# z, B, C, x and V of a hybrid layer by seven products, with their token sums held on chip

## The chip, the cores and the metric

The kernel runs on one core of a Trainium2 chip. The metric is the device time of one execution in microseconds (us), median of several runs. TensorE (PE) does matmuls and transposes; its weight loads (PEld) run beside them. VectorE (DVE), ScalarE (ACT) and GpSimd (POOL) do the elementwise work; SyncE (SP) and POOL issue the transfers between device memory (DRAM) and the on-chip memory SBUF. Matmul results land in PSUM.

## The reference

One decoder layer for 1024 tokens of 1024 features, in float32. The input is normed, projected once, and goes through two mixers side by side: a state-space scan (16 heads in 2 groups) and a differential attention (8 heads). Both outputs go through one output projection; a gated feed-forward network (FFN) and a norm follow.

```python
n   = RMSNorm(h)
p   = n @ W_in            # one combined projection, columns split into [SSD z | SSD xBC | SSD dt | DA q | DA k | DA v]
y_s = SSD(p_ssd)          # causal depthwise conv on x/B/C, chunked SSD scan, D skip, SiLU(z)-gated grouped RMSNorm
y_a = DiffAttn(p_da)      # (softmax(q1k1) - lambda softmax(q2k2)) v, causal, NoPE, per-head RMSNorm * (1 - lambda_init)
h   = h + concat(y_s, y_a) @ W_out
h   = h + SwiGLU(RMSNorm(h))
```

z and x have 1024 columns each (512 for each group), B and C 128 per group, dt 16, and q, k and v 1024 each.

## The kernel before, in words

**Exact matmuls in three.** A float32 operand is split into a high part (a copy to the PE's own float type, on ACT, L172) and a low part (the rest, a subtraction on DVE, L173). `mm3` (L126 to L129) multiplies high by high, high by low and low by high into one PSUM sum. In the trace one such product is three lines, L127, L128 and L129.

**The prologue.** Eight tiles of 128 tokens are loaded, normed (L111 on DVE; for every second tile a part of the work on POOL, L108, and ACT), transposed (16 turns of four 128x128 transposes, L120) and split (L123 on ACT, L124 on DVE) into `nhi` and `nlo`: four tiles that stay in SBUF until attention's last projection.

**Stages.** (1) z of group 0 together with dt, in units of 264 columns (`proj_z0`), then the decays. (2) For each group: B, C and four tiles of x (`conv_tiles`, by `proj_T`: 128 columns stationary, 512 tokens moving), a convolution over four tokens on DVE and a SiLU; the scan's inputs CT, Bn, CB and xn stay in SBUF. (3) The scan over eight chunks of 128 tokens (`ssd_scan`), which is mostly DVE and ACT work; on PE z of group 1 (`proj_nat`: 128 tokens stationary, 256 columns moving) runs beside scan 0, and the first V, K and Q beside scan 1. (4) Attention: for each head `qk` (K and Q by `proj_T`), for each pair of heads `v_pair` (V by `proj_nat`), and for each head eight steps, one per query block: `att_front` (scores, mask L587, maximum L588, exponential L590, reciprocal L593, the combination L596), and one step later `att_back` (transposes, the product with V at L611). A step's elementwise chain goes DVE, ACT, DVE; PE fills its wait with projections of later heads. (5) The output projection, in four groups of 512 rows; its operand is loaded from DRAM, scaled by a column of `pcol` and split by ACT and DVE (L175, L176). (6) The FFN, whose gate, up and down products already use Winograd's scheme of seven half-size products for eight.

**Order.** The program lists the work stage by stage, and the language's scheduler then orders each engine's instructions by its own timeline, once, when the kernel is built (L1077). Pools with a fixed number of buffers limit it: `B16` 4, `A4` 14, `P4` 6, `CV` 4, `raw` 2, `wh` 3, `wl` 3, and two PSUM tiles each for `MM`, `SC` and `MS`.

Of the kernel before, what the change touches and what calls it, by code (L numbers as in the profile page):

```python
# [9 lines left out]
F32 = mybir.dt.float32  # L10
# [14 lines left out]
def tile_hybrid_block(  # L25
# [51 lines left out]
    cs_d = dram.tile([P, P], F32, name="cs_d")  # L77

# [15 lines left out]
    def norm_rows(parts, wbc, outs, name, pool=(), junk=None):  # L94
        """outs = RMSNorm of the row whose column pieces are parts; pieces in pool are weighted on Pool and scaled on ACT"""
# [16 lines left out]

    def norm_transpose(parts, wbc, his, los, t, xn, pts, name, pool=()):
        norm_rows(parts, wbc, [xn], name, pool)
        tk = slice((t % 4) * P, (t % 4) * P + P)
        for q in range(2):
            pt = pts([P, 4, P], f"pt_{name}_{q}")
            for j in range(4):
                k = q * 4 + j
                nc.tensor.transpose(pt[:, j, :], xn[:, k * P:(k + 1) * P], ident)  # L120
            hi = his[t // 4][:, q * 4:q * 4 + 4, tk]
            lo = los[t // 4][:, q * 4:q * 4 + 4, tk]
            nc.scalar.copy(hi, pt)  # L123
            nc.vector.tensor_tensor(lo, pt, hi.bitcast(F32), op=ALU.subtract)  # L124
# [45 lines left out]
    def split(hi, lo, raw, scale=None):  # L170
        if scale is None:
            nc.scalar.copy(hi, raw)  # L172
            nc.vector.tensor_tensor(lo, raw, hi.bitcast(F32), op=ALU.subtract)  # L173
# [84 lines left out]
    def proj_z0(us, name, sink):
        """units of 264 columns; sink(t, psum [128 tokens, 264])"""
        for t in range(NT):  # L260
            ps = (MS if t % 4 > 1 else MM)([P, 264], f"mm_{name}_{t}")
            tk = slice((t % 4) * P, (t % 4) * P + P)
            for k in range(KD):
                hi, lo = us[k // 4]
                mm3(ps, nhi[t // 4][:, k, tk], nlo[t // 4][:, k, tk], hi[:, k % 4, :], lo[:, k % 4, :],
                    k == 0, k == KD - 1)
            sink(t, ps)

    def proj_nat(col, name, sink):
        """256 columns; sink(t, psum [128 tokens, 2 blocks from t, 256])"""  # L270
        us = [w_unit(w_in_k[:, 4 * u:4 * u + 4, col:col + 256], [P, 4, 256], f"{name}_{u}") for u in range(2)]
        for t in range(0, NT, 2):
            ps = MM([P, 2, 256], f"mm_{name}_{t}")
            for i in range(2):
                tk = slice(((t + i) % 4) * P, ((t + i) % 4) * P + P)
                for k in range(KD):
                    hi, lo = us[k // 4]
                    mm3(ps[:, i, :], nhi[t // 4][:, k, tk], nlo[t // 4][:, k, tk], hi[:, k % 4, :], lo[:, k % 4, :],
                        k == 0, k == KD - 1)
            sink(t, ps)  # L280

# [14 lines left out]
    def decays():  # L296
# [13 lines left out]
        for c in (15, 13, 11, 9, 7, 5, 3):  # L310
# [6 lines left out]
                                       op0=ALU.mult, op1=ALU.mult)  # L317
        cps = MS([P, P], "cps")
# [16 lines left out]
    def conv_tiles(*tiles):  # L335
        jobs = []
        for ct, name, acc in tiles:
            u_ = CV([P, T], F32, "u_" + name)
# [4 lines left out]

        def sink_of(ct, name, acc, u_):
            def sink(half, ps):
                sl = slice(half * 512, half * 512 + 512)
# [4 lines left out]
        for ct, name, acc, u_ in jobs:
            for sh in (1, 2, 3):
                nc.vector.scalar_tensor_tensor(acc[:, sh:], u_[:, :T - sh], wk(ct, 3 - sh), acc[:, sh:],
                                               op0=ALU.mult, op1=ALU.add)
            nc.scalar.activation(acc, acc, AF.Silu)

    def gate_dt():
        """the gate of group 0 and dt"""
        for a in range(2):
            zt = [None]  # L360
            w0, w = (0, 248) if a == 0 else (248, 264)

            def sink(t, ps):
                if t % 2 == 0:
                    zt[0] = CV([P, 2, w], F32, f"zt0_{a}_{t}")
                if a == 0:
                    nc.vector.tensor_tensor(adt[:, t, :], ps[:, 0:16], hv[:, 0, :], op=ALU.add)
                nc.scalar.activation(zt[0][:, t % 2, :], ps[:, 264 - w:], AF.Silu)
                if t % 2 == 1:
                    nc.gpsimd.dma_start(z_d[t - 1:t + 1, :, w0:w0 + w].rearrange("t p c -> p t c"), zt[0])  # L370
            proj_z0(zus if a == 0 else [z0_unit(z0_raw(1, u), 1, u) for u in range(2)], f"z0_{a}", sink)

    def gate(g):
        for hf in range(2):
            zt = [None]
            zc = g * 512 + hf * 256

            def sink(t, ps):
                if t % 4 == 0:
                    zt[0] = CV([P, 4, 256], F32, f"zt{g}_{hf}_{t}")  # L380
                nc.scalar.activation(zt[0][:, t % 4:t % 4 + 2, :], ps, AF.Silu)
                if t % 4 == 2:
                    nc.gpsimd.dma_start(z_d[t - 2:t + 2, :, zc:zc + 256].rearrange("t p c -> p t c"), zt[0])
# [698 lines left out]
```

## Time and profile before

| what | value |
|---|---|
| median of 3 runs | 1643.95 us (1643.94 to 1646.22) |
| span of the profiled execution | 1643.3 us |
| PE busy | 1597.2 us, 97% |
| DVE busy | 1071.6 us, 65% |
| ACT busy | 775.8 us, 47% |
| POOL busy | 429.2 us, 26% |
| moved by DMA | 172.78 MB, 105 GB/s |

The profile lists groups of instructions by line, engine and tile: `out<-in`, the form, `x` count, then busy time and mean ns of one, then the idle time of the engine ahead of them and what ended it. `L127 PE MATMUL mm_z<-wh_z,nhi` is the first third of z's product. A window row gives, for a stretch of the span, the busy time of each engine with its instructions, the clock that PE was granted (1.00 is full), and the DMA engines' share. In time order the stages lie at 0 to 75 us (norm, z0, dt), to 151 (B, C, x of group 0), to 228 (scan 0 with z1), to 302 (B, C, x of group 1), to 395 (scan 1 with the first V, K and Q), to 718 (attention with projections) and to 865 (attention without projections, and the output projection's start).

### The profile page before, as it was taken

The page shows a single profiled execution, that of the slowest core. Times are in us where ns is not written, and L with a number is a line of the kernel's source. Part 1 is how long each engine was busy: PE and PEld are TensorE (multiplying, and loading weights), DVE is VectorE, ACT ScalarE, POOL GpSimd, SP SyncE. Part 2 cuts the span into 40 slices and gives each one's busy share as a digit, 9 for nine tenths or more (in the row PEclk, how much of TensorE's full clock was granted, in tenths as well). Part 3 has the DMA queues.
Part 4 walks back from the last instruction along what each step waited for, and adds up shares of the span by engine and source line. Part 5 has one row for each costly group of instructions (what it writes and reads, how often), then busy time and mean ns, then how long its engine had stood idle before and what let it go on. Part 6 is the DMA issues. An engine that isn't in the chain of part 4 may idle for free. (4 is left out here: it accounts for less than half of the span.)

```text
span 1643.3 us, 23716 instructions
## 1 busy us (share of the span) xinstructions
PE 1597.2 (97%) x9170; PEld 1386.9 (84%) x9170; DVE 1071.6 (65%) x1682; ACT 775.8 (47%) x1608; POOL 429.2 (26%) x378
## 2 busy tenths in 40 slices
PE   6999999999999999999999998999999999999997
PEld 6988878887989989889999987888888888778885
DVE  5345745688776676677674477455555555898987
ACT  6444764456555565575552245333333333334445
POOL 4100330032000000013300034444444443542322
PEclk9999999999999999999999999999999999999999
DMA  5321451143011110147523221233333323944122
GB/s 195 110 79 52 129 163 56 36 142 92 24 46 39 46 33 27 45 130 229 162 77 116 84 99 56 96 102 104 111 116 118 98 96 134 365 166 186 39 103 103
DMA packets 105291, 172.78 MB, mean 105 GB/s; under 512 B 7813, under 2 KB 75530, under 8 KB 103770
## 3 DMA queue, kind: packets, MB, share of 16 engines
q1 hardware_dynamic: 95210, 137.11, 25.2%
q0 software_dynamic: 9968, 34.15, 6.3%
q8 instruction: 72, 1.18, 0.3%
q14 instruction: 41, 0.34, 0.1%
HBM read 125.82 MB, written 45.42 MB: 104 GB/s over the span
## 5 line engine op out<-in xcount | busy, mean ns | idle before, releaser
L127 PE MATMUL x<-n,wa 128*128 128x512 f32 x352 | 138.7, 396 | 0.0
L128 PE MATMUL x<-n,wa 128*128 128x512 f32 x352 | 138.7, 394 | 0.0
L129 PE MATMUL x<-n,wa 128*128 128x512 f32 x352 | 137.8, 394 | 0.0
L590 ACT ACTIVATE p<-s,nmx 128x256 f32<-128x256 f32 (+7 forms) x128 | 94.4, 740 | 53.2 <-DVE nmx L588 49.9
L172 ACT CAST wa<-s 128x512 fp32r<-128x512 f32 x88 | 54.7, 622 | 132.3 <-PE x L129 59.4
L173 DVE TENSOR_TENSOR wa<-s,wa 128x512 fp32r<-128x512 f32 x88 | 76.8, 873 | 51.1 <-ACT wa L172 50.8
L172 ACT CAST dg<-gd 128x512 fp32r<-128x512 f32 x77 | 47.7, 620 | 114.7 <-PE dx L129 57.2
L588 DVE TENSOR_REDUCE nmx<-s 128x1 f32<-128x256 f32 (+7 forms) x128 | 95.3, 754 | 2.4
L173 DVE TENSOR_TENSOR dg<-gd,dg 128x512 fp32r<-128x512 f32 x77 | 66.2, 862 | 23.3 <-ACT dg L172 23.2
L129 PEld LDWEIGHTS x<-n,wa 128*128 128x128 f32 x352 | 66.5, 189 | 15.1
L128 PEld LDWEIGHTS x<-n,wa 128*128 128x128 f32 x352 | 66.6, 189 | 14.8
L127 PEld LDWEIGHTS x<-n,wa 128*128 128x128 f32 x352 | 66.6, 189 | 14.8
L127 PE MATMUL mm_z<-wh_z,nhi 128*128 128x264 f32 (+1 forms) x256 | 75.9, 298 | 2.3 <-ACT wh_z L172 2.3
L611 PE MATMUL o<-v,p 128*128 128x128 f32 x576 | 77.7, 275 | 0.0
L129 PE MATMUL mm_z<-wh_z,nlo 128*128 128x264 f32 (+1 forms) x256 | 77.3, 303 | 0.0
L611 PEld LDWEIGHTS o<-v,p 128*128 128x128 f32 x576 | 73.5, 191 | 2.7
L128 PE MATMUL mm_z<-wl_z,nhi 128*128 128x264 f32 (+1 forms) x256 | 75.0, 294 | 0.0
L127 PE MATMUL mm_v<-wh_v,nhi 128*128 128x256 f32 x256 | 74.2, 290 | 0.0
L129 PE MATMUL mm_v<-wh_v,nlo 128*128 128x256 f32 x256 | 74.1, 290 | 0.0
L128 PE MATMUL mm_v<-wl_v,nhi 128*128 128x256 f32 x256 | 73.5, 287 | 0.0
L128 PE MATMUL po_a<-wl_wo,yh 128*128 128x256 f32 x256 | 72.6, 283 | 0.0
L91 POOL TENSOR_TENSOR rs_o<-ms_o,mhalf 128x4 f32<-128x4 f32 x16 | 18.0, 1125 | 208.4 <-DVE ms_o L89 208.3
(331 smaller groups left out, 5172.9 us busy)
## 6 DMA issues: line engine op xcount, KB each, us to landing
gd<-g_d SPq DMA_DIRECT2D x11, 1792.0 KB, 7.8
wr_g<-in_w_gate_dram SPq DMA_DIRECT2D x22, 512.0 KB, 3.8
wr_u<-in_w_up_dram SPq DMA_DIRECT2D x22, 512.0 KB, 4.3
g_d<-sg SPq DMA_DIRECT2D x22, 512.0 KB, 5.1
wr_d<-in_w_down_dram SPq DMA_DIRECT2D x22, 512.0 KB, 5.0
L<-cs_d POOLq DMA_DIRECT2D x16, 512.0 KB, 4.4
wr_y<-yT_d SPq DMA_DIRECT2D x16, 512.0 KB, 3.8
wr_wo<-in_w_out_dram SPq DMA_DIRECT2D x16, 512.0 KB, 3.5
```

Of the source, the lines that this page charges most:

```text
L91: nc.gpsimd.tensor_tensor(r, ms, mhalf[:, :w], op=ALU.pow)
L127: nc.tensor.matmul(ps, lh, rh, start=first, stop=False, skip_group_check=more)
L128: nc.tensor.matmul(ps, lh, rl, start=False, stop=False, skip_group_check=more)
L129: nc.tensor.matmul(ps, ll, rh, start=False, stop=last, skip_group_check=more)
L172: nc.scalar.copy(hi, raw)
L173: nc.vector.tensor_tensor(lo, raw, hi.bitcast(F32), op=ALU.subtract)
L588: nc.vector.reduce_max(nmx[:, m:m + 1], s[:, :Lk], axis=AX.X, negate=True)
L590: nc.scalar.activation(p[:, :Lk], s[:, :Lk], AF.Exp, bias=nmx[:, m:m + 1], accum_out=sm[:, m:m + 1])
L611: nc.tensor.matmul(o, wT[:, j * P:(j + 1) * P], vt[h % 2][j], start=(j == 0), stop=(j == i))
```

## The change

z, V, B, C and x are computed by the seven products that the FFN already uses (`in_pair`). A product pairs a sum of weight blocks with a sum of token blocks. The seven token sums, transposed and split, are made once in the prologue and stay in SBUF: four in the `B16` tiles, three in twelve of the fourteen `A4` tiles. The weight sums (four per pair of columns) are made on POOL. z and V go in wide pairs of 512 columns, B, C and x in narrow pairs of 256.

- The norm is wholly on DVE (L114) and in place; 16 token sums follow on DVE (L168), and 28 turns instead of 16.
- dt, 16 columns, is a product of its own (`dt_cols`): 40 matmuls with 32 or 16 columns stationary and 512 tokens moving, and 8 small transposes.
- All of B, C and x of both groups are computed before scan 0. The scan's inputs go to DRAM (`xn_d`, `bc_d`) and come back chunk by chunk; V goes to `v_d` and is loaded head by head (`load_v`).
- Scan 0 is interleaved with z1 and both halves of V by `weave`. After it one operand, "12", is rebuilt from x (four turns more); `plain` finds K's and Q's plain operand of four token blocks among operands 1, 2, "12" and 3.
- The column scale is applied when y is written out (on ACT); the output projection's low part is made on POOL instead of DVE. The stores of z and y go from POOL's queue to SP's.

The diff, cut to its core (`...` marks what is left out):

```diff
-    nhi = [B16([P, KD, 512], f"nhi{i}") for i in range(2)]
-    nlo = [B16([P, KD, 512], f"nlo{i}") for i in range(2)]
+    dst = {p: room(p, False, "nn") for p in (1, 2, 6, 3)}
+    dst.update({p: room(p, True, "nn") for p in (5, 7, 4)})
     for t in range(NT):
-        norm_transpose([xs[t]], mixw, nhi, nlo, t, (CV if t % 2 else P4)([P, DM], F32, f"xm_{t}"), SC, f"n{t}",
-                       (0,) if t % 2 else ())
...
+        r = norm_rows([xs[t]], mixw, [xs[t]], f"n{t}", (), SC([P, DM], f"xj{t}"))
+        if t > 3:
+            nc.vector.tensor_copy(rs4[:, t - 4:t - 3], r)
+        else:
+            turn(1, t, xs[t][:, J1], dst[1], MS, "n")
+            turn(2, t, xs[t][:, J2], dst[2], MS, "n")
+    t2s = []
+    for u in range(4):
+        x0, x1 = xs[u], xs[u + 4]
+        t2 = hx.tile([P, 512], F32, tag="hx", name=f"nt2_{u}")
+        sub(x0[:, J1], x1[:, J1], x0[:, J1], eng=nc.vector)
+        sub(t2, x1[:, J2], x0[:, J1], eng=nc.vector)
+        turn(6, u, t2, dst[6], MS, "n")
+        sub(x0[:, J2], x0[:, J2], t2, eng=nc.vector)
+        sub(x1[:, J1], x1[:, J2], x1[:, J1], eng=nc.vector)
+    for p, src in ((5, lambda u: xs[u][:, J1]), (7, lambda u: xs[u + 4][:, J1]), (3, lambda u: xs[u + 4][:, J2]),
+                   (4, lambda u: xs[u][:, J2])):
+        for u in range(4):
+            turn(p, u, src(u), dst[p], MS, "n")
...
+    def plain(half, k):
+
+        hl = ops[(1 if k < 4 else 2) if half == 0 else ("12" if k < 4 else 3)]
+        return hl[0][k % 4], hl[1][k % 4]
...
+    def in_pair(a, s5, name, wide, outs, sink, scale=None):
+
+        sub(s5, a[1][0], a[1][1], ALU.add)
+        sub(a[1][0], a[0][0], a[1][0])
...
+        for p in ORDER:
...
+            elif p == 6:
+                sub(a[0][0], s5, a[0][0])
...
+            elif p == 3:
+                sub(a[0][1], a[0][1], a[0][0])
+            src = {1: a[0][0], 2: a[0][1], 6: a[0][0], 5: s5, 7: a[1][0], 3: a[0][1], 4: a[1][1]}[p]
...
+                    split(at[:, 0], at[:, 1], src[:, k0:k0 + 2, :])
+                    for b in range(4):
...
+                            mm3(pb, bh[k][:, tk], bl[k][:, tk], at[:, 0, k - k0, :], at[:, 1, k - k0, :],
+                                new and k == 0 and b % 2 == 0, k == 3, True)
...
+                split(at[:, 0], at[:, 1], src)
+                for k in range(4):
+                    mm3(ps[0], at[:, 0, k, :], at[:, 1, k, :], bh[k], bl[k], new and k == 0, k == 3, True)
...
+    def dt_cols():
...
+                    nc.tensor.matmul(ps, w[:, kk, :], bh[k], start=q == 0 and k == 0, stop=False, skip_group_check=True)
+                    nc.tensor.matmul(ps[0:16, :], w[:, kk, 0:16], bl[k], start=False,
+                                     stop=q == len(jobs) - 1 and k == 3, skip_group_check=True)
...
+    weave([(lambda: wide_pair(C_Z + 512, "z1", sink_z(1)), 14),
+           (lambda: wide_pair(C_V, "v0", sink_v(0)), 14),
+           (lambda: wide_pair(C_V + 512, "v1", sink_v(1)), 14)], ssd_scan(0), 30 / 42)
...
+    def load_v(h):
+        v = CV([P, NT, P], F32, f"v{h}")
+        nc.sync.dma_start(v, v_d[:, :, h * P:h * P + P].rearrange("t p c -> p t c"))
+        return [v[:, j, :] for j in range(NT)]
...
     for h in range(NH):
-        if h % 2 == 0:
-            vt = v_pair(h // 2)
-        ops = qk(h)
+        vt = load_v(h)
+        kq = qk(h)
...
-            split(yh[:, j, :], yl[:, j, :], load_raw(yT_d[kt], [P, T], f"y{kt}"), scale=pcol[:, col:col + 1])
+            split(yh[:, j, :], yl[:, j, :], load_raw(yT_d[kt], [P, T], f"y{kt}"), nc.gpsimd)
```

Two places in the order of instructions. The first is DVE in the prologue, before, around the seventh norm: `nlo` are the operand's low parts, `wl_z0` a weight's low part.

```order
L111 SCALAR_TENSOR_TENSOR xm_6_281<-x_6_130,rs_n6_286,mixw_110 128x1024
L124 TENSOR_TENSOR nlo0_136<-pt_n2_0_191,nhi0_134 128x4x128
L124 TENSOR_TENSOR nlo0_136<-pt_n2_1_198,nhi0_134 128x4x128
L367 TENSOR_TENSOR adt_344<-mm_z0_0_1_377,hv_335 128x16
L224 COPY pcol_76<-pps_331 128x69
L173 TENSOR_TENSOR wl_z0_1_0_576<-wr_z0_1_0_573,wh_z0_1_0_575 128x1056
```

The same engine after the change, up to the weights of the third product, 6: L168 are token sums (`x_` tiles and `nt2`), L197 low parts of operand 6 (`nn_6`), L163 the weight's low part (`wa_z0_6`).

```order
L168 TENSOR_TENSOR nt2_2_304<-x_6_132,x_2_120 128x512
L168 TENSOR_TENSOR x_6_132<-x_6_132 128x512
L168 TENSOR_TENSOR nt2_3_316<-x_7_134,x_3_122 128x512
L168 TENSOR_TENSOR x_7_134<-x_7_134 128x512
L168 TENSOR_TENSOR x_2_120<-x_2_120,nt2_2_304 128x512
L341 TENSOR_TENSOR o_z0_00_546<-y_z0_549,o_z0_00_546 128x1024
L168 TENSOR_TENSOR x_3_122<-x_3_122,nt2_3_316 128x512
L197 TENSOR_TENSOR nn_6_142<-pt_n6_2_307,nn_6_142 128x4x128
L197 TENSOR_TENSOR nn_6_142<-pt_n6_3_319,nn_6_142 128x4x128
L163 TENSOR_TENSOR wa_z0_6_0_608<-wr_z0_00_124,wa_z0_6_0_608 128x512
```

Where z0's second weight unit came between the operand's low parts of token rows 2 and 3, the third product's first weight part now comes behind the sums of all eight rows; on PE all matmuls of products 1 and 2 stand ahead of it. The four weight sums of z0 on POOL (`s5_z0`, `wr_z0`) follow the last norm's small operations there directly:

```order
L94 TENSOR_TENSOR rs_n7_276<-ms_n7_274,mhalf_77 128x1
L168 TENSOR_TENSOR s5_z0_487<-wr_z0_10_136,wr_z0_11_138 128x1024
L168 TENSOR_TENSOR wr_z0_10_136<-wr_z0_00_124,wr_z0_10_136 128x1024
L168 TENSOR_TENSOR wr_z0_00_124<-s5_z0_487,wr_z0_00_124 128x1024
L168 TENSOR_TENSOR wr_z0_01_130<-wr_z0_01_130,wr_z0_00_124 128x1024
```

The second place is PE in attention, head 2, at its last query blocks. Before (L585 and L586 are scores, L611 the product with V, `mm_v2` and `mm_k4` projections):

```order
L585 MATMUL s2_7_1_4880<-KS2_0_4470,QH2_1_4571 128x512
L586 MATMUL s2_7_1_4880<-KS2_0_4470,QL2_1_4572 128x512
L585 MATMUL s2_7_1_4880<-KS2_1_4500,QH2_1_4571 128x512
L586 MATMUL s2_7_1_4880<-KS2_1_4500,QL2_1_4572 128x512
L127 MATMUL mm_v2_6_5558<-wh_v2_1_5401,nhi1_135 128x256
L128 MATMUL mm_v2_6_5558<-wl_v2_1_5402,nhi1_135 128x256
L129 MATMUL mm_v2_6_5558<-wh_v2_1_5401,nlo1_137 128x256
L611 MATMUL o2_5_4852<-v1_0_4225,p2_5_1_4793 128x128 x4
L127 MATMUL mm_k4_0_5615<-nhi0_134,wh_k4_5611 128x512
```

After (L766 and L767 are the scores, L788 the transposes, L792 the product with V, L805 the transposes of a finished output):

```order
L792 MATMUL o2_4_5517<-v2_5145,p2_4_1_5456 128x128 x5
L766 MATMUL s2_7_0_5579<-KS2_0_5178,QH2_1_5279 128x512
L767 MATMUL s2_7_0_5579<-KS2_0_5178,QL2_1_5280 128x512
L766 MATMUL s2_7_0_5579<-KS2_1_5208,QH2_1_5279 128x512
L767 MATMUL s2_7_0_5579<-KS2_1_5208,QL2_1_5280 128x512
L788 MATMUL wtp2_5_0_5550<-ident_72,p2_5_0_5492 128x128 x4
L788 MATMUL wtp2_5_4_5556<-ident_72,p2_5_0_5492 128x128 x2
L792 MATMUL o2_5_5560<-v2_5145,p2_5_1_5501 128x128 x6
L805 MATMUL otp2_0_5570<-ident_72,o2_0_5338 128x128 x4
```

Matmuls of V and K stood between the scores of one block and the product of an earlier one; these rows have none. Of the 42 steps from the first to the last one that a projection can stand beside, 15 have none in the new order; the other 27 have projections of K or Q.

More of the change, by code (lines that the diff above doesn't have):

```diff
@@ L111, in norm_rows @@
                 nc.vector.scalar_tensor_tensor(o, p, r, wi, op0=ALU.mult, op1=ALU.mult)
[L113 to L124, printed above, removed]
+        return r
     def mm3(ps, lh, ll, rh, rl, first, last, more=False):
@@ new lines, in tile_hybrid_block, with room @@
+    J1, J2 = slice(0, 512), slice(512, 1024)
+    ORDER = (1, 2, 6, 5, 7, 3, 4)
+    ops = {}
+    def room(p, early, name="n2"):
+        if early:
+            ts = [A4([P, 2, 512], F32R, f"{name}_{p}_{i}") for i in range(4)]
+            ops[p] = [[ts[2 * e + k // 2][:, k % 2, :] for k in range(4)] for e in range(2)]
+            return [[ts[2 * e + k] for k in range(2)] for e in range(2)]
+        bt = B16([P, 2, 4, 512], f"{name}_{p}")
+        ops[p] = [[bt[:, e, k, :] for k in range(4)] for e in range(2)]
+        return [[bt[:, e, :, :]] for e in range(2)]
@@ new lines, in turn @@
+    def turn(p, u, src, dst, bank, name="f"):
+        pt = bank([P, 4, P], f"pt_{name}{p}_{u}")
+        for k in range(4):
+            nc.tensor.transpose(pt[:, k, :], src[:, k * P:(k + 1) * P], ident)
+        n = len(dst[0])
+        w = 4 // n
+        for k in range(n):
+            hi, lo = [dst[e][k][:, :, u * P:u * P + P] for e in range(2)]
+            nc.scalar.copy(hi, pt[:, w * k:w * k + w, :])
+            nc.vector.tensor_tensor(lo, pt[:, w * k:w * k + w, :], hi.bitcast(F32), op=ALU.subtract)
@@ L254, in proj_T @@
                 for k in range(KD):
-                    mm3(ps, hi[:, k, :], lo[:, k, :], nhi[half][:, k, :], nlo[half][:, k, :], k == 0, k == KD - 1)
+                    mm3(ps, hi[:, k, :], lo[:, k, :], *plain(half, k), k == 0, k == KD - 1)
                 sink(half, ps)
[L258 to L267, printed above, removed]
@@ L283, in tile_hybrid_block, with pair_T @@
+    def pair_T(col, name, sink, scale=None):
+        a = raw_pair(col, name)
+        s5 = hx.tile([P, 4, P], F32, tag="hx", name="s5_" + name)
+        o = [CV([P, T], F32, f"o_{name}_{i}") for i in range(2)]
+        views = [[o[i][:, J1], o[i][:, J2]] for i in range(2)]
+        return in_pair(a, s5, name, False, views, lambda i, half: sink(i, half, o[i]), scale)
     W16 = [P, NT, 16]
@@ L373, in gate @@
[L373 to L383, printed above, removed]
-            proj_nat(C_Z + zc, f"z{g}_{hf}", sink)
@@ L391, in ssd_inputs, with turn_to @@
+    bcs = {}
+    def turn_to(src, o, name):
+        ov = o.rearrange("p (t c) -> p t c", c=P)
         for q in range(2):
-            pt = MS([P, 4, P], f"btp{g}_{q}")
+            pt = MS([P, 4, P], f"{name}_{q}")
             for j in range(4):
-                nc.tensor.transpose(pt[:, j, :], BT[:, (4 * q + j) * P:(4 * q + j + 1) * P], ident)
-            nc.vector.tensor_copy(Bn[:, 4 * q:4 * q + 4, :], pt)
-        CB = A4([P, NT, P], F32, f"CB{g}")
-        for q in range(2):
-            pt = MS([P, 4, P], f"cbp{g}_{q}")
-            for j in range(4):
-                ck = slice((4 * q + j) * P, (4 * q + j + 1) * P)
-                nc.tensor.matmul(pt[:, j, :], BT[:, ck], CT[:, ck], start=True, stop=True)
-            nc.scalar.copy(CB[:, 4 * q:4 * q + 4, :], pt)
@@ L413, in ssd_inputs @@
-        prev = None
-        for j in range(4):
-            xc = CV([P, T], F32, f"xc{g}_{j}")
-            conv_tiles((g * 4 + j, f"x{g}_{j}", xc))
-            if prev is not None:
-                turn(j - 1, prev)
-            prev = xc
-        turn(3, prev)
-        return CT, Bn, CB, xn
+                nc.tensor.transpose(pt[:, j, :], src[:, (4 * q + j) * P:(4 * q + j + 1) * P], ident)
+            (nc.vector.tensor_copy if q else nc.scalar.copy)(ov[:, 4 * q:4 * q + 4, :], pt)
+        return ov
@@ new lines, in sink_bc, with sink @@
+    def sink_bc(which):
+        def sink(i, half, o):
+            if (i, half) not in ((0, 1), (1, 0)):
+                return
+            acc = bcs[which, i] = conv((8 if which == "B" else 10) + i, f"{which}{i}", o)
+            bview = bc_d[i].rearrange("t p w c -> p t w c")
+            if which == "B":
+                nc.sync.dma_start(bview[:, :, 1, :], turn_to(acc, o, f"btp{i}"))
+                return
+            nc.sync.dma_start(bview[:, :, 0, :], acc.rearrange("p (t c) -> p t c", c=P))
+            ov = o.rearrange("p (t c) -> p t c", c=P)
+            for q in range(2):
+                pt = MS([P, 4, P], f"cbp{i}_{q}")
+                for j in range(4):
+                    ck = slice((4 * q + j) * P, (4 * q + j + 1) * P)
+                    nc.tensor.matmul(pt[:, j, :], bcs["B", i][:, ck], acc[:, ck], start=True, stop=True)
+                nc.scalar.copy(ov[:, 4 * q:4 * q + 4, :], pt)
+            nc.sync.dma_start(bview[:, :, 2, :], ov)
+        return sink
```

368 lines of the change are left out of this document (226 added, 142 removed).

## The prediction

> **What bounds the kernel now.** I read the page's totals first, then its forty slices, then a table of busy times by stage.
>
> ```profile
> span 1643.3 us, 23716 instructions
> PE 1597.2 (97%) x9170; PEld 1386.9 (84%) x9170; DVE 1071.6 (65%) x1682; ACT 775.8 (47%) x1608; POOL 429.2 (26%) x378
> ...
> PE   6999999999999999999999998999999999999997
> DVE  5345745688776676677674477455555555898987
> ```
>
> PE is busy for 97% and idle only in the first slice (6), a little in one of 8 and in the last (7). DVE stands at 65% on average but at 7 in many slices of the first half, the half that changes. The span, 1643.3 us, lies 0.65 us under the median of the runs, 1643.95; I make the sum against the span and add that at the end.
>
> The stages, from the view by windows (busy microseconds, instructions, granted clock, DMA share, GB/s): the norm and z0; B, C and x of group 0; scan 0 with z1; B, C and x of group 1; scan 1 with V0, K0, Q0 and K1; attention with the other K, Q and V; the attention's tail and the start of the out-projection.
>
> ```profile
> core 0: us, PE busy (x) PEld busy (x) DVE busy (x) ACT busy (x) POOL busy (x), PEclk, DMA share, GB/s
> 0.00:75.00 75.00, 59.91 (x450) 58.79 (x451) 33.81 (x64) 38.65 (x63) 22.24 (x26) 0.98 0.46 149
> 75.00:151.00 76.00, 76.00 (x371) 63.35 (x371) 34.90 (x38) 36.10 (x59) 4.29 (x7) 1.00 0.25 76
> 151.00:228.00 77.00, 72.89 (x531) 64.81 (x530) 57.37 (x84) 52.33 (x107) 25.88 (x28) 0.98 0.37 119
> 302.00:395.00 93.00, 90.95 (x553) 76.38 (x553) 77.87 (x123) 52.77 (x122) 21.75 (x28) 1.00 0.31 97
> 395.00:718.00 323.00, 323.00 (x2041) 290.03 (x2040) 222.64 (x436) 190.62 (x470) 17.01 (x21) 1.00 0.15 45
> ```
>
> The reader should see two things. Attention has PE full for 323.00 of 323.00 us with DVE at 69%: a matmul removed there is time removed, as long as something else keeps PE fed. And the prologue is the one stage with real PE idle, 15.1 of 75 us. DMA is under half busy everywhere here, so the new trips of V, x, B and C through DRAM find room; I cost them at nothing, with up to 5 us if a load at a chunk's head comes late.
>
> **The PE ledger.** Prices of one streamed matmul come from windows in which PE does one kind without a pause: 264 columns, 256 columns, 512 columns.
>
> ```profile
> 36.00:75.00 39.00, 39.00 (x325) 39.00 (x324) 13.42 (x32) 14.85 (x26) 4.37 (x7) 1.00 0.30 95
> 880.00:920.00 40.00, 40.00 (x340) 40.00 (x340) 20.03 (x23) 9.76 (x9) 0.00 (x0) 1.00 0.39 123
> 1120.00:1160.00 40.00, 40.00 (x176) 32.78 (x175) 21.06 (x27) 13.91 (x24) 17.46 (x13) 1.00 0.31 99
> ...
> 20.00 1.03 PE L120 MATMUL pt_n<-ident,xm 128*128 128x128 f32 x8
> L127 PE MATMUL mm_q<-nhi,wh_q 128*128 128x512 f32 x108 | 42.9, 398 | 0.0
> ```
>
> So .120, .118 and .228 us; a transpose is about .109 (a run of 8 rows). Seven products for eight save an eighth: z0 goes from 384 matmuls at .120 to 336 at .118 (-6.4), z1 loses 48 at .118 (-5.7), V 96 (-11.3), and x, B and C lose 72 at .228 (-16.4): -39.8 together. Against this dt now costs 40 matmuls of its own with 512 columns moving and only 32 or 16 columns stationary. No row has that form: from below, 40 at the .118 of half the columns is 4.7; from above, 40 at 398 ns, a 512-column one by itself (L127), is 16. I take .228, since the columns streamed are the same: +9.1, and +.5 for 8 small transposes. 16 turns more (12 in the prologue, four when one operand is rebuilt) are 64 transposes, +7.0. **Net -23.2 us.**
>
> **The prologue: +16.** Before, half of z0 can start when four token rows are normed. Now products 1 and 2 can, but the third, product 6, needs sums of all eight rows, and the DVE order puts 16 sums, all eight norms, 12 low parts, five weight parts and one add ahead of its weights.
>
> ```profile
> 6.99 1.28 DVE L111 SCALAR_TENSOR_TENSOR xm<-x,rs_n,mixw 128x1024 f32<-128x1024 f32 x1 [0.67 <-POOL rs_n L91]
> 19.55 2.40 POOL L108 TENSOR_TENSOR xm<-x,mixw 128x1024 f32<-128x1024 f32 x1
> 19.61 3.42 DVE L111 SCALAR_TENSOR_TENSOR xm<-x,rs_n,mixw 128x1024 f32<-128x1024 f32 x1 [0.77 <-POOL rs_n L91]
> L124 DVE TENSOR_TENSOR nlo<-pt_n,nhi 128x512 fp32r<-128x512 f32 x16 | 10.8, 687 | 12.9 <-ACT nhi L123 12.9
> L755 DVE TENSOR_TENSOR xf<-xf 128x512 f32<-128x512 f32 x4 | 2.7, 687 | 0.3 <-POOL t L755 0.3
> 1107.14 0.69 DVE L858 TENSOR_TENSOR sg<-sg,x 128x512 f32<-128x512 f32 x1 [0.49 <-PE x L129]
> 1107.76 1.29 POOL L755 TENSOR_TENSOR gs<-sg,sg 128x512 f32<-128x512 f32 x1
> 1107.84 1.75 DVE L173 TENSOR_TENSOR wa<-s,wa 128x512 fp32r<-128x512 f32 x1
> 23.00:28.20 5.20, 1.28 (x9) 0.86 (x8) 4.41 (x9) 2.50 (x3) 5.03 (x5) 1.00 0.00 1
> 28.20:36.00 7.80, 7.73 (x53) 7.73 (x53) 4.22 (x10) 4.63 (x7) 0.90 (x1) 0.78 0.26 69
> ```
>
> Eight norms at 1.28 are 10.2, 16 sums at .687 11.0, 12 low parts at .687 8.2, five splits 3.5, an add of 1,024 elements about 1.3, small ones 1.5: 35.7 us from 7.0. POOL's four weight sums of 1,024 elements fall in the same stretch. Beside POOL's 2.40 us the norm on DVE took 3.42 instead of 1.28, and beside 1.29 a split took 1.75 instead of about .69, while an op that reads PSUM kept its .69. So DVE loses about .8 of POOL's time when both its inputs are in SBUF: of 4 x 2.4 = 9.6 us I take 7 (bounds 0 and 9.6). The Trainium skill ("GPSIMD Engine Reference", section 8, Key points) says that GpSimd shares its SBUF interfaces with VectorE and contends with DVE instructions that have two SBUF inputs; it speaks against putting sums on both engines at once, and the rows above agree with it.
>
> With 3.3 us of waits at the start, product 6 can begin at 7.0 + 35.7 + 7 + 3.3 = 53 us. PE, starting at 20 as now, has ten turns (4.4) and 96 matmuls (11.3), and is out of work at 36. After 53 come five products of 48 matmuls (28.3) and 16 turns (7.0), and a colder start: after the 5.2 us above with PE nearly idle, the next 7.8 had a clock of .78, which loses 1.7. z0 ends at 90, dt at 99.6, where the stage took 75: +24.5, of which 8.4 (dt 9.6, 12 turns 5.2, z0 -6.4) are in the ledger. **+16**; from 4, if sums and splits slot in ahead of the order's worst, to 22.
>
> **Attention: +11.** V no longer lies between the steps, and K0 to Q1 and K2 go into scan 1. The order then has 15 of 42 steps (a step is one query block of one head) without any projection on PE, in runs of one to three; before it every step has some.
>
> ```profile
> L588 DVE TENSOR_REDUCE nmx<-s 128x1 f32<-128x256 f32 (+7 forms) x86 | 62.8, 740 | 1.8
> L596 DVE SCALAR_TENSOR_TENSOR p<-p,rr,p 128x256 f32<-128x256 f32 (+7 forms) x43 | 34.6, 804 | 1.5
> L587 DVE TENSOR_TENSOR s<-s,cneg 128x128 f32<-128x128 f32 x85 | 24.5, 295 | 25.7 <-PE s L586 24.6
> L595 DVE TENSOR_SCALAR rr<-r,neglam,sm 128x1 f32<-128x1 f32 x43 | 11.7, 272 | 1.4
> L593 DVE RECIPROCAL r<-sm 128x2 f32<-128x2 f32 x43 | 7.1, 164 | 41.1 <-ACT p L590 40.9
> L618 DVE TENSOR_TENSOR o<-o,rs_o 128x512 f32<-128x512 f32 x10 | 6.9, 687 | 2.8 <-POOL rs_o L91 2.8
> L127 PE MATMUL mm_v<-wh_v,nhi 128*128 128x256 f32 x192 | 54.9, 286 | 0.0
> L127 PE MATMUL mm_k<-nhi,wh_k 128*128 128x512 f32 x96 | 38.3, 399 | 0.0
> ...
> DVE r L593 <- ACT p L590: 40.9, 31, 4.1
> ```
>
> DVE's own work of 43 steps is 62.8 + 34.6 + 24.5 + 11.7 + 7.1 + 6.9 = 147.6 us, 3.43 a step. PE's: V, K and Q have three such lines each, so 576 at .118 and 612 at .228, 207.5 of the 323 us; 115.5 remain, 2.69 a step. A step without a projection is paced by DVE, .74 us behind PE; 15 of them are 11 us. From below 0: a step's scores run ahead of it, so DVE may catch up in the covered steps. By my count DVE would be at about 85% of the stage (PE's 323 less 68 of V and 24.5 of the K and Q moved forward is 231 us; DVE's 222.6 less about 16 and 10 for the same is 197), which leaves little for catching up. Scan 1, with K and Q for cover instead of V and DVE at 84% already, I put at +3 (0 to 6).
>
> Two windows with DVE that dense point both ways:
>
> ```profile
> 320.00:360.00 40.00, 40.00 (x235) 32.90 (x234) 36.05 (x53) 19.55 (x48) 10.93 (x14) 1.00 0.36 118
> 720.00:760.00 40.00, 37.66 (x298) 35.95 (x297) 34.73 (x64) 26.36 (x60) 11.82 (x15) 1.00 0.59 188
> ```
>
> At 90% in scan 1, with projections beside it, PE lost nothing; at 87% in the attention's tail, where the cover is gone, it lost 2.3 of 40.
>
> **The rest: 0.** The middle of B, C and x has DVE at half (34.9 of 76), which covers the conversion to seven products; scan 0 gets V and z1 as cover, more than before. In the out-projection 16 low parts go from DVE (about 1.3 each) to POOL (about 2.4 each, 38 us in all); the loads lie a group ahead, so this is hidden: if not, one late group costs 2 to 4 us. The scale by the column moves to evictions on ACT, which is at half.
>
> **Sum:** -23.2 + 16 + 11 + 3 = +7; with 1643.95, **1651 us**.
>
> **Rivals.**
> *Attention stays covered.* The window at 320 speaks for it, the one at 720 against. Then 1651 - 11 = 1640 (1635 to 1644). Chance .24.
> *The prologue is covered too* (its stall 4 instead of 16): 1628. The DVE order speaks against it, since 16 sums cannot be done before row 7 is normed. Chance .08.
> *DVE and ACT pace the bare steps one after the other.* Place: the 15 steps without a projection, and it decides once two follow each other, since then no matmul fills the wait of L593 for the exponentials. The wait list has 31 of those at 1.3 us mean, now hidden behind V's matmuls. Bare, they add 15 x 1.3 = 20: 1671, clearly slower. Against it: scores of the next step overlap. Chance .14.
> By the Trainium skill ("TensorE: Matmul & The Clock Gate", What's actually happening) an idle window of some 3.4 us halves the clock. The row at 28.2 (.78 after 5.2 us nearly idle) agrees; pauses in attention of .74 a step, or 2.2 over three, stay below the gap seen there, so it would add nothing to attention.
> *The products do not save what they count*, because narrow dt matmuls cost 16 instead of 9, or the split parts arrive too late in x: +7 or more, 1658. Chance .04.
>
> **How the numbers follow.** My forecast, both stalls, has .50 and its own range, 1643 to 1660. The range of 1633 to 1668 leaves out the covered prologue, most of the third rival and a tail of each other, 2 in 10. A measurement of this kernel tells .2% (3.3 us) from no change. Faster than 1640.7: .08 and half of the .24, and .06 of the forecast's low tail: .26. Same: the other half of .24 with .09 of the forecast: .21. Slower: .35 + .14 + .04 = .53.
>
> **What would show it.** Prologue: PE idle in a block of some 16 us between about 36 and 53, ended by DVE's split of product 6's first weights; z0 done near 90. If that block is under 8 us, this step is wrong. Attention: PE below 97% with the idle ended by L588 or L596's successors, in the steps without K or Q; if PE stays at 100% there, I am wrong by 11. Ledger: PE's busy time should be near 1597 - 23 = 1574, and the stretch of the six pairs of B, C and x should take some 17 us less than the two stretches now. A dt line of mean above .3 us would break the 9.1. What would make it wrong altogether is a load of a scan chunk or of V that PE waits for.

## The result, and the profile after

The changed kernel takes 1701.23 us (1697.38 to 1705.87, 4 runs), the kernel before 1645.09 beside it: a ratio of 1.0347, 95% interval 1.0322 to 1.0373. It is slower by 56 us, outside the range.

The page of the changed kernel: totals, then PE, DVE and the granted clock in forty slices.

```profile
span 1699.7 us, 23930 instructions
PE 1598.4 (94%) x9018; PEld 1379.0 (81%) x9018; DVE 1160.9 (68%) x1775; ACT 816.5 (48%) x1721; POOL 516.0 (30%) x402
...
PE   5999989999988998988999998999999999999997
DVE  8666787776877667677676358655455555698987
...
PEclk9899999998999999999999999999999999999999
```

Where PE had nines from slice 2 to slice 24, six slices up to the 19th now show an 8. Its busy time did not fall by 23 us, as the ledger has it, though 152 fewer matmuls are recorded: a matmul counts as busy for longer when the clock is low (one of K took .63 us at 413 us, where the clock was .64, and .39 at 418), and when it follows a pause (.50 at 405). The stages, by windows, with the columns of the first table: scan 0 with z1 and V; operand 12, scan 1 and the first K and Q; attention; its tail and the output projection; the rest.

```profile
230.00:397.00 167.00, 158.18 (x1214) 148.92 (x1212) 128.01 (x152) 96.99 (x215) 53.42 (x39) 0.98 0.56 176
397.00:510.00 113.00, 102.62 (x485) 80.49 (x484) 82.75 (x137) 61.61 (x152) 16.68 (x23) 0.94 0.46 130
510.00:780.00 270.00, 243.48 (x1344) 205.62 (x1344) 188.12 (x383) 173.91 (x443) 26.50 (x24) 0.98 0.13 40
780.00:988.00 208.00, 201.82 (x1629) 197.53 (x1630) 126.05 (x224) 94.97 (x221) 66.83 (x62) 1.00 0.43 142
988.00:1699.00 711.00, 691.42 (x3254) 577.01 (x3252) 475.50 (x660) 269.84 (x496) 291.85 (x208) 0.99 0.35 123
```

With the boundaries set at the first matmul of the output projection (718.3 us before, 779.9 after) and at its last of the first three groups (920.5 and 985.9), the account is this:

| stretch | by the prediction | measured |
|---|---|---|
| norm, z0, dt, all of B, C and x | 233 | 230 |
| scan 0 with z1 and V | 151 | 167 |
| scan 1 and attention with K and Q | 341 | 383 |
| attention's tail and output projection | 202 | 206 |
| the rest, mostly FFN | 723 | 714 |

The first is right; the loss lies in the scans and above all in attention, and the FFN, whose code hardly changed, is 9 us shorter. The list of PE's waits in the changed kernel:

```profile
PE s L766 <- ACT p L771: 17.3, 23, 2.0
PE pt_n L191 <- DVE nt L168: 8.8, 2, 4.4
...
PE wtp L788 <- DVE p L777: 6.0, 6, 1.7
PE o L792 <- ACT p L789: 5.3, 10, 1.0
PE yp L615 <- DVE y L604: 3.8, 3, 1.9
```

The scores waited 17.3 us for exponentials; before, that row had 2.9:

```profile
PE s L585 <- ACT p L590: 2.9, 3, 1.7
```

One bare stretch at the end of a head, in the timeline of PE (start, length, instruction, and in brackets the idle time ahead of it with what ended it):

```profile
638.51 0.50 PE L766 MATMUL s<-KS,QH 128*128 128x512 f32 x1 [0.43 <-ACT p L771]
...
640.83 1.60 PE L792 MATMUL o<-v,p 128*128 128x128 f32 x12 [0.46 <-ACT p L789]
...
645.95 1.83 PE L792 MATMUL o<-v,p 128*128 128x128 f32 x14 [0.51 <-ACT p L789]
...
649.76 0.39 PE L766 MATMUL s<-KS,QH 128*128 128x256 f32 x1 [1.81 <-ACT p L771]
```

and its last two steps as windows:

```profile
638.51:645.00 6.49, 5.78 (x37) 4.58 (x37) 5.88 (x9) 4.97 (x14) 0.60 (x1) 1.00 0.00 0
645.00:649.76 4.76, 2.44 (x18) 2.16 (x19) 4.14 (x10) 4.67 (x11) 0.00 (x0) 1.00 0.15 57
```

Here DVE is busy for 5.88 of 6.49 us and 4.14 of 4.76, ACT for 4.97 and 4.67, and PE waits for the exponentials that free the two score buffers and for the copies of the transposed weights, all of it ACT's work. DVE is not the pace alone, as I had it. Nor is ACT only waiting for DVE: ahead of the longest wait shown, 1.81 us, DVE had the maximum ready at 646.6, and ACT first wrote out parts of K and Q of later heads (`QH`, `KS`), whose matmuls lie in other steps:

```profile
646.35 0.27 DVE L769 TENSOR_REDUCE nmx<-s 128x1 f32<-128x128 f32 x1
...
647.40 0.62 ACT L746 CAST QH<-QH 64x512 fp32r<-64x512 f32 x1
648.03 0.58 ACT L733 CAST KS<-mm_k 64x512 fp32r<-64x512 f32 x1
648.63 0.59 ACT L743 ACTIVATE QH<-mm_q 64x512 fp32r<-64x512 f32 x1
649.25 0.37 ACT L771 ACTIVATE p<-s,nmx 128x128 f32<-128x128 f32 x1
```

I cut the timeline at the first scores of each step, from 509.7 to 776.9 us. Of these 41 steps 16 have no projection. They take 82.1 us, PE idles for 21.4 of them, DVE is busy for 71.5 and ACT for 71.9, and the busier of the two in each step adds up to 76.7. In the other 25 steps, 185.1 us, PE idles for 3.0. By an estimate of PE's work (.2247 us for 512 columns, in proportion for fewer, .11 for a 128x128 transpose or product with V) the bare steps lose 32 us, 2.0 each. The others lose 16, of which about 7 are the clock; the kernel before loses 8 in its 41 steps by the same estimate.

The clock adds to it. Windows of 3.4 us in attention:

```profile
694.20:697.60 3.40, 2.61 (x22) 2.27 (x20) 2.95 (x6) 3.36 (x8) 0.04 (x1) 1.00 0.20 77
697.60:701.00 3.40, 1.68 (x9) 1.36 (x10) 2.86 (x7) 3.27 (x10) 0.00 (x0) 0.94 0.00 0
701.00:704.40 3.40, 3.40 (x13) 2.83 (x12) 2.71 (x8) 2.13 (x8) 0.00 (x0) 0.56 0.02 5
704.40:707.80 3.40, 3.40 (x19) 2.87 (x17) 0.00 (x0) 0.00 (x0) 0.00 (x0) 1.00 0.00 0
...
592.20:595.60 3.40, 1.47 (x12) 1.12 (x10) 3.34 (x5) 3.32 (x7) 0.60 (x1) 1.00 0.12 47
595.60:599.00 3.40, 3.14 (x14) 2.60 (x15) 2.99 (x8) 3.31 (x9) 0.00 (x0) 1.00 0.08 30
```

From 697.6 us PE was busy for half of a window, in short pauses, and in the next the clock was .56. From 592.2 it was busy for less, and the next window had 1.00. Two more such windows, both with PE busy for 1.59 us, went one way each: after the one at 748.6 the clock was .53, after the one at 646.6 it was 1.00. So it can follow and need not; these windows do not show what decides.

### The profile page after: what moved, and what is told of

The parts are those of the page before. It is cut to its first block, busy times and chain, and to the rows that moved or that the text cites. A ratio compares the mean times of both kernels' runs of the same rounds, so it can differ in the third digit from the quotient of the medians.

```text
span 1699.7 us, 23930 instructions
## 1 busy us (share of the span) xinstructions
PE 1598.4 (94%) x9018; PEld 1379.0 (81%) x9018; DVE 1160.9 (68%) x1775; ACT 816.5 (48%) x1721; POOL 516.0 (30%) x402
## 5 line engine op out<-in xcount | busy, mean ns | idle before, releaser
L163 DVE TENSOR_TENSOR wa<-s,wa 128x512 fp32r<-128x512 f32 x88 | 76.6, 872 | 48.4 <-ACT wa L162 48.2
L766 PE MATMUL s<-KS,QH 128*128 128x512 f32 (+2 forms) x192 | 71.8, 376 | 17.5 <-ACT p L771 17.3
L792 PE MATMUL o<-v,p 128*128 128x128 f32 x576 | 78.0, 277 | 5.4 <-ACT p L789 5.3
L792 PEld LDWEIGHTS o<-v,p 128*128 128x128 f32 x576 | 72.6, 191 | 10.0 <-ACT p L789 7.8
L163 DVE TENSOR_TENSOR dg<-gd,dg 128x512 fp32r<-128x512 f32 x77 | 63.5, 828 | 22.5 <-ACT dg L162 22.4
L768 DVE TENSOR_TENSOR s<-s,cneg 128x128 f32<-128x128 f32 x128 | 37.5, 294 | 53.6 <-PE s L767 49.8
L118 PE MATMUL po_a<-wh_wo,yh 128*128 128x256 f32 x256 | 73.4, 287 | 0.0
L120 PE MATMUL po_a<-wh_wo,yl 128*128 128x256 f32 x256 | 72.8, 284 | 0.0
L119 PE MATMUL dx<-dw,dg 128*128 128x512 f32 x176 | 67.9, 392 | 2.9 <-DVE dw L163 2.8
L118 PE MATMUL z<-n,wa 128*128 128x512 f32 x176 | 68.6, 390 | 0.0
```

Source lines behind the costliest of these rows:

```text
L118: nc.tensor.matmul(ps, lh, rh, start=first, stop=False, skip_group_check=more)
L119: nc.tensor.matmul(ps, lh, rl, start=False, stop=False, skip_group_check=more)
L120: nc.tensor.matmul(ps, ll, rh, start=False, stop=last, skip_group_check=more)
L163: eng.tensor_tensor(lo, raw, hi.bitcast(F32), op=ALU.subtract)
L766: nc.tensor.matmul(sc, QH[i // 4][:, m, qr], KS[c][:, m, :w], start=True, stop=False)
L768: nc.vector.tensor_tensor(s[:, qs], s[:, qs], cneg, op=ALU.add)
```

## The experiments

The theories: A, attention needs projections between its steps, and V was that cover; B, attention is long for another reason that came with the change; C, POOL's weight sums stretch DVE's work, against D, DVE's own load is the pace; E and F, on the shorter FFN; G and H, on operand 12.

**V alone, taken out of attention in the kernel before.**

```diff
     gate(1)
+    for hh in range(NH // 2):
+        proj_nat(C_V + hh * 256, f"v{hh}", sink_v)     # evicted by DVE, stored to v_d
     ssd_scan(1, *ssd_inputs(1))
...
-        if h % 2 == 0:
-            vt = v_pair(h // 2)
+        vt = load_v(h)
```

> The kernel before with one thing changed: all of V is computed ahead of scan 1 by the old products, kept in DRAM and loaded head by head; its PE work is the same. Theory A (cover): attention then has 14 bare steps, each paced by the chain of elementwise work, and loses 2 to 2.7 us in each: 1645 + 28 to 38 = about 1678, with 25 us or more of PE idle in attention. Theory B (attention's loss comes from what else changed: K and Q on the new operands, the seven products' buffers, a colder start): no change, 1640 to 1650.

Measured: 1695.46 us, ratio 1.0320 (1.0302 to 1.0338). With no seven products, no token sums and the same matmuls, moving V costs 53 us against the 1642.41 beside it. Its attention:

```profile
488.00:768.30 280.30, 249.29 (x1364) 208.48 (x1362) 195.94 (x400) 177.90 (x454) 17.11 (x21) 0.98 0.15 47
```

31 us of PE idle. K and Q have 511 matmuls here by the groups, 116.5 us at .228, and with attention's own 115.5 that is 232 us of work in 280: 48 lost, 3.4 for each of 14 bare steps. Not all of it lies in them: with the same cut by steps, about half falls in bare steps and the rest in steps with some projections left, where about 7 us are the clock. B falls; A holds, with a price above what it expected.

**V undone in the changed kernel.**

```diff
-           (lambda: wide_pair(C_V, "v0", sink_v(0)), 14),
-           (lambda: wide_pair(C_V + 512, "v1", sink_v(1)), 14)], ssd_scan(0), 30 / 42)
+           ], ssd_scan(0), 30 / 14)
...
-        vt = load_v(h)
+        if h % 2 == 0:
+            vp = v_pair(h // 2)      # 256 columns by three matmuls each, from operands 1, 2, 12 and 3
+        vt = vp[h % 2]
```

> The changed kernel with V undone: V is computed plainly per pair of heads inside attention, as before; z, B, C and x stay on seven products. V costs 11.3 us more of PE. Theory A: attention has two bare steps left, its 40 us of loss shrink to 5 and scan 1 has V for cover again (10 us less): 1701 + 11 - 35 - 10 = 1667 (1655 to 1678). Theory B: 1712.

Measured: 1678.58 us, ratio 1.0216 (1.0201 to 1.0231): 23 us faster than the changed kernel, with 11 us more of matmuls, but 12 us short of A's 1667, just past the end of its range. The windows of scan 0, scan 1 and attention say where:

```profile
229.00:356.00 127.00, 107.65 (x699) 94.22 (x698) 96.30 (x130) 77.24 (x180) 36.33 (x32) 0.85 0.62 194
356.00:450.00 94.00, 93.21 (x540) 77.88 (x539) 75.25 (x127) 55.33 (x141) 16.87 (x22) 1.00 0.35 101
450.00:763.00 313.00, 307.91 (x1914) 275.17 (x1912) 205.58 (x410) 185.98 (x459) 26.46 (x24) 0.99 0.14 42
```

Attention is full again (5 us idle of 313) and so is scan 1. Scan 0 now has z1 alone beside it, since V must wait for operand 12: PE idles 19 us there, and its clock falls to .85. The bare place moved.

**Half of V undone.** The second `wide_pair` of V goes from `weave`, and heads 4 to 7 use `v_pair` as above.

> The changed kernel with half of V undone: heads 0 to 3 keep seven products beside scan 0, heads 4 to 7 are computed plainly inside attention; 8 bare steps instead of 15. Theory A: half of attention's loss goes, V costs 5.7 more: 1701 + 6 - 20 = 1687 (1678 to 1694). Theory B: 1707.

Measured: 1684.78 us, ratio 1.0251 (1.0221 to 1.0281), as A has it.

**Work added for nothing.**

```diff
         kq = qk(h)
+        for d in range(6 if 1 <= h <= 5 else 0):
+            ps = MM([P, 512], f"dm{h}_{d}")
+            for k in range(16):
+                nc.tensor.matmul(ps[:, 0:256], plain(0, k % 8)[0][:, 0:P], plain(1, k % 8)[0][:, 0:256],
+                                 start=k == 0, stop=k == 15)
```

> The changed kernel with work added that nothing reads: 480 matmuls of 256 columns on tiles that are in SBUF anyway, 96 in each of heads 1 to 5, 57 us of PE work at .118 each, with no work for DVE or ACT. Theory A (bare steps leave PE waiting, and the pauses lower its clock): most of it fits in the pauses: 1701 + 25 at most, so 1701 to 1726, with PE idle in the attention stretch down from 26 us to under 10 and its clock at 1.00. Theory B (the stage is long for reasons inside PE's own work): 1701 + 57 = 1758.

Measured: 1719.84 us, ratio 1.0459 (1.0445 to 1.0474): 57 us of matmuls cost 19, so two thirds fitted in what PE had lost.

```profile
510.00:797.60 287.60, 279.68 (x1726) 248.31 (x1725) 187.78 (x380) 172.70 (x435) 25.89 (x23) 0.98 0.13 40
```

The window ends at the first matmul of the output projection, as that of the changed kernel does; 96 of the 480 matmuls lie ahead of it, in scan 1. Idle fell from 26.5 us to 7.9, as A expects; the clock of the stretch stayed at .98, where A expected 1.00.

**The weight sums on DVE.**

```diff
-        sub(s5, a[1][0], a[1][1], ALU.add)
-        sub(a[1][0], a[0][0], a[1][0])
+        sub(s5, a[1][0], a[1][1], ALU.add, eng=nc.vector)
+        sub(a[1][0], a[0][0], a[1][0], eng=nc.vector)
```

and the two sums ahead of products 6 and 3 likewise.

> The changed kernel with the 40 weight sums of the in-projection moved from POOL to DVE (36 us more of DVE work). Theory C (while POOL adds, DVE's operations with both inputs in SBUF are stretched by about the same time, so POOL's help is not free): the prologue and scan 0 gain, 1701 - 5 to 12 = about 1693, and the convolution and the xd products of DVE that took 2.9 to 3.4 us between 229 and 243 us go back to 1.3 and 0.7. Theory D (DVE paces the scans by its own load): 36 us more on it cost 8 to 15, 1712.

Measured: 1689.38 us, ratio 1.0293 (1.0265 to 1.0320): 12 us faster than the changed kernel with 40 more operations on DVE. C holds against D. The start of scan 0, in the changed kernel first (DVE, and POOL's sums beside it), then with the sums on DVE:

```profile
230.28 3.43 DVE L514 SCALAR_TENSOR_TENSOR cv_x<-o_x,pcol,cv_x 128x1023 f32<-128x1023 f32 x1
233.63 2.88 DVE L589 TENSOR_TENSOR xd<-zx,dt_n 128x512 f32<-128x512 f32 x1
236.44 1.27 DVE L514 SCALAR_TENSOR_TENSOR cv_x<-o_x,pcol,cv_x 128x1022 f32<-128x1022 f32 x1
...
229.87 2.75 POOL L168 TENSOR_TENSOR wr_z<-wr_z,wr_z 128x1024 f32<-128x1024 f32 x1
232.71 3.26 POOL L168 TENSOR_TENSOR wr_z<-s_z,wr_z 128x1024 f32<-128x1024 f32 x1
```

```profile
227.68 1.23 DVE L168 TENSOR_TENSOR wr_z<-s_z,wr_z 128x1024 f32<-128x1024 f32 x1
228.83 1.28 DVE L514 SCALAR_TENSOR_TENSOR cv_x<-o_x,pcol,cv_x 128x1023 f32<-128x1023 f32 x1
230.02 0.68 DVE L589 TENSOR_TENSOR xd<-zx,dt_n 128x512 f32<-128x512 f32 x1
```

The same convolution step takes 1.28 instead of 3.43 us, the same product .68 instead of 2.88. By the marks of the two traces the last matmul of x comes 4 us earlier and the first of K 12 us earlier: 4 gained in the prologue and the stage behind it, 8 in scan 0. The sums themselves are done sooner as well, in 1.23 us on DVE instead of 2.75 and 3.26; how much of the 12 us is that, and how much the end of the stretching, this run does not separate. The Trainium skill's rule that GpSimd and VectorE contend where VectorE has two SBUF inputs ("GPSIMD Engine Reference", section 8, Key points) agrees with the stretched rows.

**Both repairs.** Sums on DVE and half of V undone.

> Both repairs in one: weight sums on DVE, and V of heads 4 to 7 computed plainly in attention. Theories A and C together, if their gains add: 1701 - 16 - 12 = 1673 (1668 to 1680). If they hide each other: 1684 or more. Neither reaches the kernel before at 1643, since heads 0 to 3 and both scans stay thinly covered.

Measured: 1683.76 us, ratio 1.0229 (1.0208 to 1.0250), no better than half of V alone within the spread. The gains hide each other: the scan's first product with its state comes 4.4 us earlier than with half of V alone (255.1 against 259.5 us), but the first matmul of K .4 later (357.1 against 356.7), so scan 0 gives back what was gained ahead of it. What PE waits for there instead stays open.

**The buffers' distance.**

```diff
-                    at = wp.tile([P, 2, 2, 256], F32R, tag="wh", bufs=3, name=f"wa_{name}_{p}_{k0}")
+                    at = wp.tile([P, 1056], F32R, tag="wh", bufs=3, name=f"wa_{name}_{p}_{k0}")[:, 0:1024].rearrange("p (a b c) -> p a b c", a=2, b=2)
```

and the same for one tile of tag wl, so that every buffer of the two tags takes 4224 bytes.

> The changed kernel with nothing changed but the distance between the buffers of split weights (tags wh and wl): 4224 bytes, as the 264-column units of the kernel before made it, instead of 4096. Theory E (the 512-column matmuls run at .2247 us after the change and at .2279 before because their weights lie on 4096-byte steps): the FFN goes from 714 back to 723 us and the whole to 1701 + 9 to 14 = 1712; the window rate in the FFN goes from 178 to 175.5 matmuls in 40 us. Theory F (the rate hangs on something else in the FFN, such as the single 512-column turn): no change, 1701.

Measured: 1709.79 us, ratio 1.0403 (1.0384 to 1.0423): 8.6 us slower for 128 bytes more in each buffer. Its FFN window, with 175 matmuls in 40 us, and that of the changed kernel, with 179:

```profile
1200.00:1240.00 40.00, 40.00 (x175) 32.68 (x174) 20.33 (x27) 12.73 (x21) 17.86 (x13) 1.00 0.32 100
```

```profile
1200.00:1240.00 40.00, 40.00 (x179) 33.10 (x178) 21.31 (x28) 12.99 (x22) 17.53 (x14) 1.00 0.31 100
```

**The same in the kernel before.**

```diff
-        hi = wp.tile([P, 4, 264], F32R, tag="wh", bufs=3, name=f"wh_z0_{a}_{u}")
-        lo = wp.tile([P, 4, 264], F32R, tag="wl", bufs=3, name=f"wl_z0_{a}_{u}")
+        hi = wp.tile([P, 4, 256], F32R, tag="wh", bufs=3, name=f"wh_z0_{a}_{u}")
+        lo = wp.tile([P, 4, 256], F32R, tag="wl", bufs=3, name=f"wl_z0_{a}_{u}")
...
             proj_z0(zus if a == 0 else [z0_unit(z0_raw(1, u), 1, u) for u in range(2)], f"z0_{a}", sink)
+            if a == 0:
+                dt_cols()      # 32 matmuls, on nhi and nlo
```

> The kernel before with z0 in units of 256 columns instead of 264, so that the weights' buffers lie 4096 bytes apart, and dt as a product of its own (32 matmuls of 512 moving columns at .225, 8 small transposes: +8; z0's narrower matmuls: -0.8). Theory E: all 512-column matmuls of the kernel gain 3 ns, some 9 us in the FFN and 4 in the projections: 1643 + 7 - 13 = 1637. Theory F: 1643 + 7 = 1650.

Measured: 1634.69 us against 1644.40, ratio .9939 (.9925 to .9952): faster than both kernels. E holds on both sides, in that the size of these buffers sets the rate; since other tiles can move with it, neither run separates the distance from the addresses. The window in its FFN:

```profile
1200.00:1240.00 40.00, 40.00 (x179) 33.10 (x178) 19.46 (x26) 12.49 (x22) 16.15 (x12) 1.00 0.35 112
```

**Operand 12's loads on another queue.**

```diff
-        nc.sync.dma_start(xt, x2[(4 + u) * P:(5 + u) * P, J1])
+        nc.gpsimd.dma_start(xt, x2[(4 + u) * P:(5 + u) * P, J1])
```

> The changed kernel with the loads from which operand 12 is rebuilt (four row tiles of x and the norm's weights) issued on POOL's queue instead of SP's. In the trace the first of them to be late leaves SP's queue at 397.7 us, behind loads of weights, gates and parameters, and PE then has a clock of .89 and .64 for 23 us. Theory G (the queue makes operand 12 late, and this costs scan 1 about 7.6 us: 2.6 of idle and 5 of clock): 1701 - 5 to 8 = 1694. Theory H (the rebuild would be late anyway, since its room is a buffer that the last product 6 frees): 1701.

Measured: 1695.91 us, ratio 1.0310 (1.0290 to 1.0331), 5 us faster, but not by what G names:

```profile
400.00:410.00 10.00, 7.80 (x40) 6.00 (x38) 5.49 (x8) 4.17 (x7) 1.14 (x2) 1.00 0.85 251
410.00:420.00 10.00, 7.72 (x24) 6.21 (x25) 6.85 (x13) 0.79 (x2) 1.09 (x1) 0.53 1.16 314
```

The pause and the low clock behind it are still there, so SP's queue was not what made the operand late: POOL issues the late load at 400.6 us, and by the trace it is a turn on PE (`pt_n`) that ends POOL's wait for it. By the marks of the two traces scan 0 ends 2.6 us later than in the changed kernel, and the stretch from the first matmul of K (400.5 us, in the changed kernel 397.9) to the first scores of head 0's fifth block (516.7, there 518.1) takes 4.0 less. Why stays open, as does what the rebuild costs by itself.

**The output projection's part alone,** on top of the faster kernel: the column scale at the writing of y, on ACT, and the low parts on POOL.

```diff
-            nc.scalar.copy(yt, pt)
+            for j in range(4):
+                nc.scalar.mul(yt[:, j, :], pt[:, j, :], pcol[:, SN + g * 4 + j:SN + g * 4 + j + 1])
...
-        nc.scalar.copy(oT, pt)
+        nc.scalar.mul(oT, pt, pcol[:, SL:SL + 1])
...
-            split(yh[:, j, :], yl[:, j, :], load_raw(yT_d[kt], [P, T], f"y{kt}"), scale=pcol[:, col:col + 1])
+            split(yh[:, j, :], yl[:, j, :], load_raw(yT_d[kt], [P, T], f"y{kt}"), nc.gpsimd)
```

> The kernel before with z0 in 256 columns (measured at .9939 of the kernel before), and of the change one more part: the scan's and attention's outputs are scaled by their column when they are written, and the output projection's low parts are made on POOL instead of DVE. My term for it was 0: same ratio, .994. If POOL's 16 subtractions of 2.4 us stretch DVE's work there, as its sums did in the prologue, or come late for a group: 2 to 6 us more, .996.

Measured: 1641.34 us, ratio .9984 (.9973 to .9994): 7 us given back. Attention's last steps lie beside it. Its window, and that of the faster kernel without the part:

```profile
800.00:850.00 50.00, 45.16 (x349) 43.02 (x348) 34.14 (x60) 25.16 (x65) 16.74 (x13) 1.00 0.41 129
```

```profile
800.00:850.00 50.00, 47.51 (x375) 45.76 (x374) 36.06 (x69) 26.63 (x70) 7.52 (x9) 1.00 0.38 121
```

POOL does 9 us more here, and PE idles 4.8 instead of 2.5 us. But the loss begins earlier: the first scores of attention come at 387.4 instead of 384.9 us, before POOL has such a low part to make, and the last group of the output projection at 924.8 instead of 919.6. In the scans y is now written by four operations a chunk instead of one, 64 of .369 us instead of 16 of .579, which is a candidate; the run does not separate the two halves, and the order of the instructions changed with them.

## Why the prediction was wrong

- **The ledger was right.** The matmuls went as counted; dt's came every .23 us (30 of them from 86.61 to 93.33), near the .228 I took for a form that no row had.
- **The prologue, +16, was right in its mechanism and 4 us too large.** DVE was busy through 20 to 47 us, POOL's sums stretched four of its own to 2.2 to 2.8 us (7.4 in all, where I took 7), product 6 ran steadily from 49.5, where I had 53, and dt was done at 96, where I had 99.6. The block of idle that I named as its sign was smaller: between 37 and 49.5 us PE idled for 7.2, and its turns there ran at a clock of .50. That an operation reading PSUM keeps its .69 beside POOL I took from a row that ends as POOL's begins; in the changed kernel one of .69 from 227.74 does lie within a sum of POOL from 227.39 to 229.79.

```profile
37.24 2.84 DVE L168 TENSOR_TENSOR x<-x 128x512 f32<-128x512 f32 x1
40.00 2.82 DVE L168 TENSOR_TENSOR nt<-x,x 128x512 f32<-128x512 f32 x1
42.75 0.68 DVE L168 TENSOR_TENSOR x<-x 128x512 f32<-128x512 f32 x1
```

- **Attention, +11, is the step that failed, on its size.** The place was right: bare steps. But I priced them at .74 us each, the mean of DVE's work over all 43 steps less that of PE's, and left ACT out. 168 projections of K and Q in three matmuls each (.2247 each at the new rate, 113 us) and 115.5 of attention's own are 229 us of work; the stage took 270: 41 us lost instead of 11, 2.7 for each of 15 steps; with V alone moved it was 3.4. By the cut into steps about 2.0 of that lies in a bare step itself: DVE has 4.5 us of work there, not 3.43, ACT as much, and PE about 3.1, and the step takes 5.1. The rest lies in the steps with projections, the low clock among it. My third rival named DVE and ACT one after the other, but added only the 20 us of one wait and had .14; it took L593's waits from a stage whose cover hid the others.
- **The clock** was dismissed since no pause would reach the 5.2 us seen in the prologue. The windows above show that half a window of short pauses can be enough. The Trainium skill speaks of "a free-running 4096-cycle activity window" ("TensorE: Matmul & The Clock Gate", What's actually happening); I had read it as a pause of that length. The clock of .98 over 270 us is about 5 us.
- **Scan 0, 0,** cost 16: I had priced POOL's effect on DVE in the prologue and did not carry it to the weight sums of z1 and V, which fall beside the scan. 8 of the 16 came back with the sums on DVE; the other 8 stay open. **Scan 1, +3,** cost about 16 (10 us idle, and 113 us at a clock of .94); which part is operand 12 stays open.
- **The output projection, 0,** cost 4 here, and its part 7 by itself. Some of the 7 is lost in the scans already, where I counted the column scale as free; how much POOL's low parts cost is not shown.
- **The FFN, 0,** gained 9. I had read .228 for 512 columns as a fixed price; it hung on the buffer size that the 264-column units had set.

## What to carry to other kernels

Before moving work away from a chain that alternates between engines, count what each engine has to do in the very steps that will be bare, those that write out the projections' results included, and not its mean over the stage: here the busier of DVE and ACT, step by step, gave 76.7 of the 82.1 us. One part alone, moved in the kernel before, gives the price directly. A second engine's "free" additions are not free where they meet the first engine's two-input operations. And a small change in a tile's size can move its neighbours too: look at the rate of unchanged code before and after.

## What was not expected of the hardware

- Matmuls of 512 columns ran 1.4% slower, 175 instead of 178 or 179 in 40 us at a granted clock of 1.00, when each buffer of their split weights took 4224 instead of 4096 bytes; putting the size in or taking it out moved two kernels by 8 to 10 us in opposite directions.
- A granted clock of .56 followed 3.4 us in which PE was busy for 1.68 us, with no recorded wait above .9 us; 3.4 us with PE busy for 1.47 was followed by 1.00.
